# A hybrid decoder layer on one core: first loads and steps in another order, key tiles in turn with the gate logits, inverse roots spread without diagonal tiles

## The chip, the core and the metric

The kernel runs on one core of a Trainium2 chip. A core has a matrix engine (TensorE, PE in the profile, with its weight loads as PEld), a vector engine (VectorE, DVE), a scalar engine (ScalarE, ACT), GpSimd (POOL) and a queue for transfers (SyncE, SP). Each works through its own list of instructions in a fixed order and waits for the others by semaphores. The metric is the device time of one launch in microseconds (us), less is better.

## The reference

One decoder layer over 1024 prompt tokens and 8 x 8 sample tokens (1088 columns in the kernel), width 1024. Two branches work on the same normalized input and are merged by sigmoid gates; an MLP and a gated projection of per-layer inputs follow. All is float32.

```python
def trunk_layer(h, p_l, ...):
    proj = rmsnorm(h, norm_mix) @ w_in
    qkv, z, b_logit, a_logit, sq, sk, sv, gates = jnp.split(proj, cuts, axis=-1)
    o_a, conv_new, s_new = gdn_branch(qkv, z, b_logit, a_logit, ...)
    o_b, k_new, v_new = swa_branch(sq, sk, sv, ...)
    gates = jax.nn.sigmoid(gates)
    mix = gates[..., :D_MODEL] * o_a + gates[..., D_MODEL:] * o_b
    h = h + mix @ w_out
    hid = jax.nn.relu(rmsnorm(h, norm_ffn) @ w_up)
    h = h + (hid * hid) @ w_down
    h = h + jax.nn.sigmoid(rmsnorm(h, norm_ple) @ w_ple_gate) * (p_l @ w_ple_proj)
...
def gdn_branch(...):      # causal conv of width 4 with silu, then the gated delta rule in chunks of 64
    beta = jax.nn.sigmoid(b_logit)
    g = -jnp.exp(a_log) * jax.nn.softplus(a_logit + dt_bias)
...
def swa_branch(...):      # 16 heads of 64, 4 key heads, window of 128, sinks
```

## The kernel before, in words

Activations lie transposed: 128 channels on the partitions, tokens along the columns, in three column chunks (`CH`) of 384, 384 and 320. Each float32 product of a weight tile is made of three matmuls in a faster float type: high x high, high x low, low x high (`gemm_steps`, lines 165 to 167). So each weight tile `wr` that is loaded is split into `wh` (ScalarE, line 133) and `wl` (GpSimd, for the first two tiles VectorE, line 134). A list `order` holds the order of the weight tiles; `next_w` keeps the load three tiles and the split two tiles ahead. Activations are split in the same way (`xh` by ScalarE at line 316, `xl` by VectorE or GpSimd at line 317; `phi` and `plo` for the per-layer inputs, line 285).

Code is written in the order of the steps, and a scheduler with its own costs then fixes each engine's list. A generator given to `side` lets other work be set between the matmuls of a tile: after every third matmul (line 168) one entry of `side` is called.

The stages in the order of time: eight tiles of the per-layer projection, `ple(0)` to `ple(7)`, 18 matmuls each, whose results are copied to `ppo` (line 327) and stored; between them, `x_norm` for each of the three chunks of x, in three steps: squares (line 305) and folds (line 308) to one column sum per partition; `rsqrt_pe`; scaling (line 315) and splitting. Then 48 matmuls for the gate logits (line 385, weight `wba`), the gate arithmetic, the eight key tiles (`conv_steps`: 72 matmuls each, then a convolution with three VectorE steps at line 508 and the key at line 519, then `key_rows` and `key_products`), the tiles of the sliding-window branch, while VectorE solves the triangular systems (`substitute`, lines 657 and 658, tiles `fs` and `LT`). Then come eight gate tiles with the attention's steps between their matmuls: scores (lines 921 and 922, from `khi`, `klo` and `qst`), spreading (944), values (966); `qst` is made at line 892 and `klo` at line 879. The recurrent heads, the output projection, the MLP and the last gate follow.

`rsqrt_pe` turns column sums into inverse roots that lie on all partitions. One-column matmuls (line 246) bring the sums of up to 128 tokens into a column of `psn`; VectorE scales them (249), GpSimd takes the power (250); for each 128 tokens VectorE makes a diagonal tile `dg` (255, two buffers), and PE spreads it by a product with ones (256). It is called for the three chunks of x, and for the three chunks at the end of the output projection and of the MLP (`col_rsqrt_pe`, where PE's L246 waits for `acc`, line 1355).

Of the kernel before, what the change touches and what calls it, by code (L numbers as in the profile page):

```python
# [17 lines left out]
P = 128  # L18
# [20 lines left out]
def hybrid_layer(ctx: ExitStack, tc: tile.TileContext, d):  # L39
# [72 lines left out]
    wst = dict(raw=[], split=[], used=0)  # L112
# [8 lines left out]
    def w_split():  # L121
        i = len(wst["split"])
        if i < len(order):
            raw, n = wst["raw"][i]
            hi = wp.tile([P, 1024], F32R, name="wh", tag="wh")
            lo = wp.tile([P, 1024], F32R, name="wl", tag="wl")
            rv, hv, lv = raw[:, :n], hi[:, :n], lo[:, :n]
            if n == 128:

                rv = rv.rearrange("p (k m) -> p k m", m=16)  # L130
                both = hi[:, :256].rearrange("p (k m) -> p k m", m=32)
                hv, lv = both[:, :, 0:16], both[:, :, 16:32]
            act(hv, rv, AF.Copy)  # L133
            (nc.gpsimd if i > 1 else nc.vector).tensor_tensor(lv, rv, hv.bitcast(F32), ALU.subtract)  # L134
            wst["split"].append((hi, lo))

    def next_w():
        i = wst["used"]
        wst["used"] += 1
        while len(wst["raw"]) < min(i + 3, len(order)):  # L140
            w_load()
        while len(wst["split"]) < min(i + 2, len(order)):
# [94 lines left out]
    def rsqrt_pe(acc, c0, w, mul, add, rb, np_):  # L237
# [14 lines left out]
        for c in range(n):  # L252
            m = min(P, w - c * P)
            dg = np_.tile([P, P], F32, name="dg", tag="dg", bufs=2)
            ts(out=dg[:m, :m], in0=ident[:m, :m], scalar1=comp[:m, c : c + 1], scalar2=None, op0=ALU.mult)
            mm(ps[:, c * P : c * P + m], ones[:m], dg[:m, :m], start=True, stop=True)
# [4 lines left out]
    def col_rsqrt_pe(acc, mul, add, rb, np_):  # L261
        for c0, w in CH:
            rsqrt_pe(acc[:, c0 : c0 + w], c0, w, mul, add, rb, np_)
# [11 lines left out]
    with ExitStack() as st:  # L275
# [5 lines left out]
        for i, (c0, w) in enumerate(CH):  # L281
# [5 lines left out]
            if i == 0 or i == 1:  # L287
                w_load()
                w_split()
        for i, (c0, w) in enumerate(CH):  # L290
# [4 lines left out]
            if i == 1:  # L295
                load_constants()
        w_load()

        def x_norm(i):
# [6 lines left out]
            n = 4  # L306
# [4 lines left out]
            rs = rsqrt_pe(sq[:, 0], c0, w, 1.0 / 1024, EPS, None, pp)  # L311
# [23 lines left out]
        for step in (0, 1, 2, n0, n1, n0, n0, 3, n1, n2, n1, 4, 5, n2, n2, 6, 7):  # L335
# [11 lines left out]
    def evac_to(dst):  # L347
        def f(c0, w, ps):
            act(dst[:, c0 : c0 + w], ps[:, :w], AF.Copy)  # L349
        return f  # L350

# [28 lines left out]
    wb, _ = next_w()  # L380
    for c0, w in CH:
        ps = pg.tile([P, 512], F32, name="ps", tag="ps")
        for k in range(KT):
            for i in range(2):
                mm(ps[:32, :w], wb[:, k * 32 : k * 32 + 32], xs[k][i][:, c0 : c0 + w], start=(k + i == 0), stop=(k + i == KT))
        act(ba[:, c0 : c0 + w], ps[:32, :w], AF.Copy)
# [93 lines left out]
    def conv_tile(f, cvp, dst):  # L480
        st = conv_steps(f, cvp, dst)
        while True:
            try:
                next(st)
            except StopIteration as e:
                return e.value

    def conv_steps(f, cvp, dst):

        raw = cvp.tile([P, RAWW], F32, name="raw", tag="raw", bufs=2)  # L490
        rs = raw[:, 3 + NP :].rearrange("p (b t) -> p b t", t=11)
        nc.gpsimd.memset(raw[:, 0:3], 0.0)
        nc.gpsimd.tensor_copy(rs[:, :, 0:3], cache[:, f])

        def evac(c0, w, ps):
            n = min(w, NP - c0)
# [1037 lines left out]
```

## Time and profile before

| | us |
|---|---|
| runs: median of three | 2181.7 |
| runs: lowest, highest | 2180.86, 2184.86 |
| profiled execution: its own time | 2175.17 |
| profiled execution: span from the first to the last instruction | 2173.4 |
| PE busy in the span | 2111.1 |
| DVE, ACT, POOL busy | 1081.9, 796.6, 706.7 |

The mean granted clock of TensorE in the span is 0.986 of full speed. In the profile, L and a number is a line of the kernel; a tile's name stands with what it is made from (`wl<-wr,wh`). A row of the timeline gives the start, the length, the engine, the line and the operation, and in brackets the time that the engine stood idle ahead of it with what ended that. Rows of windows give the busy time of each engine in a stretch of time. A matmul's length holds its way through the array; two matmuls overlap, so their cost is read from their starts.

### The profile page before, as it was taken

The numbers are of one execution on the slowest core, as the hardware profiler recorded it, in microseconds if no ns is written. First come the engines' busy times: TensorE is split into PE (matmuls) and PEld (weight loads), VectorE is DVE, ScalarE is ACT, GpSimd is POOL, SyncE is SP. The second block draws the span as 40 slices with busy tenths as digits, with TensorE's granted clock in tenths as the row PEclk, the third lists the DMA queues.
The fourth block names the chain that finished last, engine by engine and source line by source line (L and its number), as shares of the span: only waits on it lengthen the run. The fifth ranks groups of instructions, "written<-read, shape, count | busy, mean of one in ns | idle before, by whom it ended". The sixth has DMA issues, their size and how long they took to land.

```text
span 2173.4 us, 33492 instructions
## 1 busy us (share of the span) xinstructions
PE 2111.1 (97%) x13485; PEld 2010.5 (93%) x13485; DVE 1081.9 (50%) x1724; ACT 796.6 (37%) x1951; POOL 706.7 (33%) x616
## 2 busy tenths in 40 slices
PE   7999998899999999999999999999999999999999
PEld 6899998777889999999998999999999999999999
DVE  6454599776644555455545543233332323333654
ACT  6576432576643443343335223122121212212321
POOL 4333355333234444544445321212121221212121
PEclk9999999999999999999999999999999999999999
DMA  6465343432143133222332221111111111111132
GB/s 245 140 202 186 106 154 104 128 118 91 64 139 101 64 98 121 94 73 86 111 112 78 88 89 40 39 49 42 46 49 39 49 39 49 47 42 49 39 125 80
DMA packets 89575, 196.62 MB, mean 90 GB/s; under 512 B 34124, under 2 KB 45260, under 8 KB 89292
## 3 DMA queue, kind: packets, MB, share of 16 engines
q1 hardware_dynamic: 89420, 194.48, 27.6%
q8 instruction: 106, 1.74, 0.3%
q14 instruction: 49, 0.40, 0.1%
HBM read 145.61 MB, written 50.78 MB: 90 GB/s over the span
## 4 chain that ended last, share of the span: by engine, by line
PE 80%; DVE 10%; ACT 4%; issue 3%; DMA 1%; POOL 1%; SPq 0%; DVEq 0%; ACTq 0%; POOLq 0%
PE ps L165 23%; PE ps L167 22%; PE ps L166 22%; DVE fs L657 3%; DVE LT L658 2%; PE psn L966 1%; PE pst L944 1%; PE psc L1252 1%; PE pst L1232 1%; PE psc L921 1%; ACT pst L568 1%; PE psc L1247 1%; PE psc L922 1%; PE pst L1126 1%; PE psn L1264 1%
## 5 line engine op out<-in xcount | busy, mean ns | idle before, releaser
L134 POOL TENSOR_TENSOR wl<-wr,wh 128x1024 fp32r<-128x1024 f32 x140 | 343.7, 2455 | 903.8 <-ACT wh L133 903.8
L165 PE MATMUL ps<-xh,wh 128*128 128x384 f32 (+1 forms) x1800 | 626.5, 348 | 3.0 <-ACT qf L349 1.6
L166 PE MATMUL ps<-xl,wh 128*128 128x384 f32 (+1 forms) x1800 | 597.6, 332 | 0.0
L167 PE MATMUL ps<-xh,wl 128*128 128x384 f32 (+1 forms) x1800 | 594.5, 330 | 0.0
L165 PEld LDWEIGHTS ps<-xh,wh 128*128 128x128 f32 x1800 | 341.2, 190 | 26.2 <-issue 21.0
L133 ACT ACTIVATE wh<-wr 128x1024 fp32r<-128x1024 f32 x143 | 150.8, 1054 | 526.1 <-PE ps L166 444.2
L166 PEld LDWEIGHTS ps<-xl,wh 128*128 128x128 f32 x1800 | 341.7, 190 | 1.6 <-issue 0.7
L167 PEld LDWEIGHTS ps<-xh,wl 128*128 128x128 f32 x1800 | 340.6, 189 | 1.9 <-issue 0.9
L165 PE MATMUL ps<-uh,wh 128*128 128x384 f32 (+1 forms) x768 | 250.7, 326 | 1.2 <-DVE h L1403 1.2
L167 PE MATMUL ps<-uh,wl 128*128 128x384 f32 (+1 forms) x768 | 250.9, 327 | 0.0
L166 PE MATMUL ps<-ul,wh 128*128 128x384 f32 (+1 forms) x768 | 250.6, 326 | 0.0
L1403 DVE TENSOR_TENSOR h<-h,ps 128x384 f32<-128x384 f32 (+1 forms) x192 | 100.6, 531 | 226.3 <-PE ps L167 226.3
L166 PE MATMUL ps<-pl,wh 128*128 128x384 f32 (+1 forms) x600 | 197.5, 329 | 0.0
L165 PE MATMUL ps<-ph,wh 128*128 128x384 f32 (+1 forms) x600 | 197.4, 329 | 0.0
L167 PE MATMUL ps<-ph,wl 128*128 128x384 f32 (+1 forms) x600 | 197.0, 329 | 0.0
L1389 DVE TENSOR_TENSOR ul<-us,uh 128x384 fp32r<-128x384 f32 (+1 forms) x96 | 98.0, 1022 | 115.3 <-ACT uh L1388 115.3
L165 PEld LDWEIGHTS ps<-uh,wh 128*128 128x128 f32 x768 | 144.1, 188 | 2.0 <-DVE h L1403 2.0
L167 PEld LDWEIGHTS ps<-uh,wl 128*128 128x128 f32 x768 | 144.1, 188 | 0.0
L166 PEld LDWEIGHTS ps<-ul,wh 128*128 128x128 f32 x768 | 144.1, 188 | 0.0
L508 DVE SCALAR_TENSOR_TENSOR cacc<-raw,cw,cacc 128x1112 f32<-128x1112 f32 x72 | 109.5, 1521 | 62.0 <-ACT cacc L506 56.7
L1387 ACT ACTIVATE us<-ut 128x384 f32<-128x384 f32 (+1 forms) x96 | 48.2, 502 | 197.6 <-DVE ut L1386 196.1
L1386 DVE SCALAR_TENSOR_TENSOR ut<-ps,rb 128x384 f32<-128x384 f32 (+1 forms) x96 | 51.3, 535 | 138.2 <-PE ps L167 138.2
(407 smaller groups left out, 3472.1 us busy)
## 6 DMA issues: line engine op xcount, KB each, us to landing
wr<-win SPq DMA_DIRECT2D x60, 512.0 KB
wr<-wup SPq DMA_DIRECT2D x32, 512.0 KB
wr<-wdn SPq DMA_DIRECT2D x32, 512.0 KB
ppd<-ppo SPq DMA_DIRECT2D x8, 544.0 KB
kTd<-kT SPq DMA_DIRECT2D x8, 544.0 KB
Ed<-E SPq DMA_DIRECT2D x8, 544.0 KB
rg<-Ed SPq DMA_DIRECT2D x8, 544.0 KB
gkT<-kTd SPq DMA_DIRECT2D x8, 544.0 KB
```

Source lines behind the costliest of these rows:

```text
L133: act(hv, rv, AF.Copy)
L134: (nc.gpsimd if i > 1 else nc.vector).tensor_tensor(lv, rv, hv.bitcast(F32), ALU.subtract)
L165: mm(ps[:M, :w], a, h[:, c0 : c0 + w], start=(k == 0), stop=False)
L166: mm(ps[:M, :w], a, l[:, c0 : c0 + w], start=False, stop=False)
L167: mm(ps[:M, :w], b, h[:, c0 : c0 + w], start=False, stop=(k == n - 1))
L508: stt(out=cc, in0=raw[:, j : j + CONVW], scalar=cw[:, f, j : j + 1], in1=cc, op0=ALU.mult, op1=ALU.add)
L657: tt(tmp, X[:, j : j + 1, j + 1 :].broadcast_to(sh), X[:, 0:j, j : j + 1].broadcast_to(sh), ALU.mult)
L658: tt(X[:, 0:j, j + 1 :], X[:, 0:j, j + 1 :], tmp, ALU.add)
L1386: stt(out=t, in0=ps[:, :w], scalar=0.0, in1=rb2[:, c0 : c0 + w], op0=ALU.max, op1=ALU.mult)
L1387: act(s, t, AF.Square)
L1389: tt(lo[:, c0 : c0 + w], s, hi[:, c0 : c0 + w].bitcast(F32), ALU.subtract)
L1403: tt(hc, hc, ps[:, :w], ALU.add)
```

## The change

1. First loads: the order was p0, wpp0, p1, wpp1, p2, x0, x1, constants, x2; now it is p0, wpp0, p1, p2, x0, constants, wpp1, x1, the first key weight, x2. `wba` moves behind the first two key weights in `order`, and its split goes to a tile of its own (`wn`).
2. In `x_norm`, the first fold (1536 columns) is done by GpSimd for the chunks 1 and 2. The steps come in the order 0, 1, 2, n0, 3, n0, n0, 4, n1, 5, n1, 6, n1, n2, 7, n2, n2.
3. `rsqrt_pe` has no diagonal tile: the column of inverse roots is broadcast along the free dimension as one operand, and the identity is the other.
4. The first two key tiles and the logits run chunk by chunk in turn: key 0, key 1, logits for the first two chunks, logits, key 0, key 1 for the third. The gate arithmetic comes behind them.
5. The attention's steps start at slot 20 of the gate tiles' slots instead of slot 6, with a second step in each tenth slot.

```diff
-    order = [(d["wpp"][u], 1024) for u in range(2)] + [(d["wba"], 128)]
+    order = [(d["wpp"][u], 1024) for u in range(2)]
     order += [(d["win"][f], 1024) for f in WIN_ORDER]
+    order.insert(4, (d["wba"], 128))
...
-            dg = np_.tile([P, P], F32, name="dg", tag="dg", bufs=2)
-            ts(out=dg[:m, :m], in0=ident[:m, :m], scalar1=comp[:m, c : c + 1], scalar2=None, op0=ALU.mult)
-            mm(ps[:, c * P : c * P + m], ones[:m], dg[:m, :m], start=True, stop=True)
+            mm(ps[:, c * P : c * P + m], comp[:m, c : c + 1].broadcast_to([m, P]), ident[:m, :m], start=True, stop=True)
...
+        p_chunk(0)
         w_load()
+        w_split()
+        p_chunk(1)
+        p_chunk(2)
+        x_chunk(0)
+        load_constants()
+        w_load()
+        w_split()
+        x_chunk(1)
+        w_load()
+        x_chunk(2)
...
-            n = 4
+            (tt if i == 0 else nc.gpsimd.tensor_tensor)(sq[:, 0:4], sq[:, 0:4], sq[:, 4:8], ALU.add)
+            n = 2
             while n:
                 tt(sq[:, 0:n], sq[:, 0:n], sq[:, n : 2 * n], ALU.add)
                 n //= 2
...
-        for step in (0, 1, 2, n0, n1, n0, n0, 3, n1, n2, n1, 4, 5, n2, n2, 6, 7):
+        for step in (0, 1, 2, n0, 3, n0, n0, 4, n1, 5, n1, 6, n1, n2, 7, n2, n2):
...
+    wst["narrow"] = lambda: kp.tile([P, 256], F32R, name="wn", tag="kb", bufs=1)
+
+    def logit_steps():
+        wb, _ = next_w(0)
+        for c0, w in CH:
+            ps = pg.tile([P, 512], F32, name="ps", tag="ps")
+            for k in range(KT):
+                for i in range(2):
+                    mm(ps[:32, :w], wb[:, k * 32 : k * 32 + 32], xs[k][i][:, c0 : c0 + w], start=(k + i == 0), stop=(k + i == KT))
+            act(ba[:, c0 : c0 + w], ps[:32, :w], AF.Copy)
+            yield
...
+    first = [conv_steps(8 + h, kp, key_tile) for h in range(2)]
+    logits = logit_steps()
+    for i, _ in enumerate(CH):
+        for st in (*first, logits) if i < 2 else (logits, *first):
+            next(st)
...
-                if n >= 6:
+                if n >= 20:
                     next(steps, None)
+                    if n % 10 == 9:
+                        next(steps, None)
```

Three places show what the scheduler makes of it. The first is GpSimd's list at the start; `rcomp` is the column of inverse roots, `xl` the low part of a normalized x tile (`xc_139` before and `xc_133` now are chunk 0, `xc_142` and `xc_152` chunk 1), `xsq` the squares. Before:

```order
L250 TENSOR_TENSOR rcomp<-rcomp,pwr 128x3 x2
L317 TENSOR_TENSOR xl<-xc_139,xh 128x384 x4
L134 TENSOR_TENSOR wh<-wr,wh 128x8x16
L317 TENSOR_TENSOR xl<-xc_139,xh 128x384 x2
L317 TENSOR_TENSOR xl<-xc_142,xh 128x384 x5
```

and now:

```order
L253 TENSOR_TENSOR rcomp<-rcomp,pwr 128x3
L318 TENSOR_TENSOR xsq<-xsq 128x1536
L330 TENSOR_TENSOR xl<-xc_133,xh 128x384 x2
L137 TENSOR_TENSOR wl<-wr,wh 128x1024
L330 TENSOR_TENSOR xl<-xc_133,xh 128x384 x4
L253 TENSOR_TENSOR rcomp<-rcomp,pwr 128x3
L318 TENSOR_TENSOR xsq<-xsq 128x4x320
L330 TENSOR_TENSOR xl<-xc_152,xh 128x384 x5
```

The power of chunk 1 stood right behind that of chunk 0; now the fold of chunk 1, six subtractions and a weight's split stand between them.

The second is VectorE's list around the first scores of the attention, within the triangular solution (`fs` and `LT`; the last number of an `LT` row counts down as it goes on). Before:

```order
L658 TENSOR_TENSOR LT<-LT,fs 128x49x14
L657 TENSOR_TENSOR fs<-LT 128x650
L892 TENSOR_TENSOR qst<-qraw,qst 64x1024
L658 TENSOR_TENSOR LT<-LT,fs 128x50x13
L879 TENSOR_TENSOR klo<-kraw,khi 128x1024
L657 TENSOR_TENSOR fs<-LT 128x612
```

and now:

```order
L687 TENSOR_TENSOR LT<-LT,fs 128x49x14
L686 TENSOR_TENSOR fs<-LT 128x650
L687 TENSOR_TENSOR LT<-LT,fs 128x50x13
L921 TENSOR_TENSOR qst<-qraw,qst 64x1024
L686 TENSOR_TENSOR fs<-LT 128x612
L908 TENSOR_TENSOR klo<-kraw,khi 128x1024
```

`qst` and `klo` each moved one operation of the solution back. On PE, 46 matmuls of the first gate tiles stand ahead of the first score, where 27 stood.

The third is PE's list at the end of the output projection, where the inverse roots are made; `psn` takes the column sums, `pst` the spread roots, and `ps` are plain matmuls. Before:

```order
L246 MATMUL psn<-cst,acc 128x1 x2
L246 MATMUL psn<-cst,acc 64x1
L165 MATMUL ps<-ph_12657,wh 128x384
L256 MATMUL pst<-dg,cst 128x128 x2
L166 MATMUL ps<-pl_12658,wh 128x384
L256 MATMUL pst<-dg,cst 128x128 x2
L167 MATMUL ps<-ph_12657,wl 128x384
L256 MATMUL pst<-dg,cst 128x128 x2
L165 MATMUL ps<-ph_12657,wh 128x384
L256 MATMUL pst<-dg,cst 128x64
```

and now:

```order
L257 MATMUL pst<-cst,rcomp 128x128 x6
L249 MATMUL psn<-cst,acc 128x1 x2
L249 MATMUL psn<-cst,acc 64x1
L169 MATMUL ps<-pl_12546,wh 128x320
L170 MATMUL ps<-ph_12545,wl 128x320
L168 MATMUL ps<-ph_12638,wh 128x384
L257 MATMUL pst<-cst,rcomp 128x128 x2
L257 MATMUL pst<-cst,rcomp 128x64
```

The spreading matmuls stood in twos between plain ones; now six come together ahead of the last column sums, and three behind three plain matmuls.

More of the change, by code (lines that the diff above doesn't have):

```diff
@@ L135, in w_split, with next_w @@
             wst["split"].append((hi, lo))
-    def next_w():
+    def next_w(ahead=1):
         i = wst["used"]
         wst["used"] += 1
-        while len(wst["raw"]) < min(i + 3, len(order)):
+        while len(wst["raw"]) < min(i + 2 + ahead, len(order)):
             w_load()
-        while len(wst["split"]) < min(i + 2, len(order)):
+        while len(wst["split"]) < min(i + 1 + ahead, len(order)):
             w_split()
```

134 lines of the change are left out of this document (65 added, 69 removed).

## The prediction

> **What bounds the kernel now.** I read the page first, for the engine that sets the time.
>
> ```profile
> PE 2111.1 (97%) x13485; PEld 2010.5 (93%) x13485; DVE 1081.9 (50%) x1724; ACT 796.6 (37%) x1951; POOL 706.7 (33%) x616
> ```
>
> TensorE (PE) is busy for 2111.1 of 2173.4 us, so no edit that leaves its matmuls alone can win more than the 62.3 us in which it stands, plus what it loses while it is busy at a lower clock. The second view is PE's waits (what it waited for, microseconds in all, times, longest).
>
> ```profile
> PE psc L921 <- DVE qst L892: 8.2, 1, 8.2
> PE ps L165 <- ACT wh L133: 6.7, 1, 6.7
> PE pst L256 <- DVE dg L255: 3.9, 2, 3.3
> PE ps L165 <- ACT ppo L327: 3.3, 1, 3.3
> PE psc L921 <- POOL qst L892: 2.3, 1, 2.3
> PE ps L165 <- ACT phi L285: 1.7, 1, 1.7
> PE pst L432 <- DVE lg L417: 1.7, 1, 1.7
> ```
>
> The 6.7 us are the first weight's load and split; the change keeps that load in place, so they stay. The other rows are what it can reach: 8.2 and 2.3 us in the attention, the rest at the start. The third view is the same places as windows (window, its length, busy time of PE, PEld, DVE, ACT and POOL with counts; then the granted PE clock, DMA share, GB/s).
>
> ```profile
> 28.00:36.00 8.00, 4.60 (x18) 4.04 (x17) 8.00 (x13) 5.69 (x14) 7.29 (x7) 0.69 0.33 111
> 36.00:46.00 10.00, 7.57 (x43) 7.22 (x41) 8.00 (x14) 5.90 (x15) 8.03 (x9) 0.91 0.62 218
> 46.00:52.00 6.00, 5.09 (x21) 4.38 (x22) 4.91 (x12) 2.22 (x6) 1.88 (x3) 0.72 0.00 1
> 60.00:88.70 28.70, 27.02 (x167) 25.69 (x167) 16.56 (x61) 12.62 (x38) 6.72 (x8) 1.00 0.25 80
> 367.00:376.00 9.00, 0.78 (x5) 0.49 (x4) 8.80 (x9) 0.69 (x1) 3.27 (x2) 0.79 0.00 0
> 420.00:440.00 20.00, 15.68 (x96) 12.68 (x96) 13.12 (x29) 10.23 (x29) 10.10 (x5) 0.74 0.42 120
> 1297.00:1311.00 14.00, 13.41 (x61) 12.12 (x60) 3.98 (x14) 1.42 (x3) 2.94 (x4) 0.63 0.09 34
> 2069.00:2081.00 12.00, 10.96 (x56) 9.90 (x55) 4.10 (x14) 1.42 (x3) 2.94 (x4) 0.72 0.35 134
> ```
>
> The window from 60 to 88.7 holds the gates' matmuls and the first two key tiles. Two things are lost in the others: idle time, and time at a clock of about a half. The two blocks of inverse roots (the last two rows) show almost no idle time: they lose by the clock, and by small matmuls that wait their turn. The fourth view is PE's own timeline at the start (start, length, what, and in brackets the wait ahead).
>
> ```profile
> 12.61 0.59 PE L165 MATMUL ps<-phi,wh 128*128 128x320 f32 x2 [1.69 <-ACT phi L285]
> 13.21 0.34 PE L167 MATMUL ps<-phi,wl 128*128 128x384 f32 x1
> 13.38 0.34 PE L165 MATMUL ps<-phi,wh 128*128 128x384 f32 x1
> ...
> 32.13 0.69 PE L165 MATMUL ps<-phi,wh 128*128 128x384 f32 x1 [3.35 <-ACT ppo L327]
> ...
> 34.54 0.52 PE L165 MATMUL ps<-phi,wh 128*128 128x384 f32 x1
> 34.86 0.52 PE L166 MATMUL ps<-plo,wh 128*128 128x384 f32 x1
> ...
> 46.90 0.68 PE L256 MATMUL pst<-dg,cst 128*128 128x128 f32 x4 [3.33 <-DVE dg L255]
> ```
>
> Starts of 384-column matmuls lie 0.17 us apart after the wait of 1.69 us, and 0.32 apart after the one of 3.35: the longer wait costs its own length and then some microseconds at half speed. In the Trainium skill, "TensorE: Matmul & The Clock Gate", Part 1, the clock halves after about one idle window of 3.4 us that runs freely; the 3.35 and 1.69 fit that, but the block at 1297 does not, since it shows a clock of 0.63 with 0.6 us idle. I therefore go by the granted clock of the rows.
>
> What the start loses now, by these rows: waits 1.7 + 3.35 + 3.33 + 1.7 = 10.1 us. The clock of 0.69 in 8 us and 0.91 in 10 us is (0.31 x 8 + 0.09 x 10) / 0.5 = 6.8 us at half clock, about 1.1 of them before the restart at 32.13, so some 5.7 us of work lost half its speed, 2.8 us; 0.72 in 6 us is 3.4 us, 1.7 lost. Together about 14.6 us.
>
> **The change part by part.**
>
> **First loads, POOL's fold, and the first steps.** These rows carry the costs (DVE's, then POOL's timeline).
>
> ```profile
> 20.58 1.75 DVE L308 TENSOR_TENSOR xsq<-xsq 128x1536 f32<-128x1536 f32 x1
> 26.58 1.66 DVE L315 SCALAR_TENSOR_TENSOR xc<-xc,par,pst 128x384 f32<-128x384 f32 x3
> 28.16 0.55 DVE L317 TENSOR_TENSOR xl<-xc,xh 128x384 fp32r<-128x384 f32 x1
> ```
>
> ```profile
> 20.75 2.31 POOL L250 TENSOR_TENSOR rcomp<-rcomp,pwr 128x3 f32<-128x3 f32 x1 [20.32 <-DVE rcomp L249]
> 25.49 0.85 POOL L250 TENSOR_TENSOR rcomp<-rcomp,pwr 128x3 f32<-128x3 f32 x1 [2.44 <-DVE rcomp L249]
> 39.32 5.22 POOL L317 TENSOR_TENSOR xl<-xc,xh 128x384 fp32r<-128x384 f32 x5 [1.97 <-ACT xh L316]
> 52.92 2.40 POOL L134 TENSOR_TENSOR wl<-wr,wh 128x1024 fp32r<-128x1024 f32 x1 [0.41 <-ACT wh L133]
> ```
>
> The third chunk of p now lands ahead of x0, and ScalarE copies it before x0's squares: the 1.69 us wait goes. The next thing late is x0. PE finishes tiles 0 to 3 at about 21 (72 matmuls of 0.16 from 6.65, with the first dozen at half speed), then has three column sums and stands for the power on POOL: 0.85 us if alone, 2.31 if it meets VectorE as at 20.75; I take 0.85.
>
> Tile 4 then runs to about 26.2, and after it PE's order has the column sums of x1, with its spreading matmuls right behind, ahead of tiles 5 to 7, which need neither. PE is in order, so 54 ready matmuls stand behind x1. Its first fold is now on POOL. No row shows that fold there: DVE takes 1.75 us for it, and POOL's 2.40 for 1024 columns makes 3.6 for 1536; I take 3.6, POOL's own rate. From about 23.4, where I lay the end of x1's squares (the constants are now loaded ahead of it), that ends at 27.0. The two remaining folds (each a part of 1.75: 0.9 and 0.5) are behind x0's eight scalings (8 x 0.55) and two subtractions (2 x 0.55) on DVE, 5.5 us from 23.9, so they end at about 30.8: PE waits some 4.5 us. Then the power of x1 has to wait on POOL behind six subtractions of x0 (5.22 / 5 = 1.04 each) and a weight's split (2.40), 8.7 us from 27.0, and ends about 36: PE stands another 4.3 us after its sums. x2's power costs a further 1.2 or so. Waits: 0.85 + 4.5 + 4.3 + 1.2 = 10.9 us, and about 2.3 us lost to half clock behind the middle two, as before behind one such wait. That is 13.2 against 12.9 before (14.6 without the gate chain's 1.7): the new order makes about as much standing time as it takes away. A second count, by stages, is kinder: laying tiles 5 to 7, then the 192 matmuls of two key tiles and the logits behind these waits, I reach about 82.6, to which the gates' matmuls, now behind, add about 4 with the 1.7 us wait; before, the same work was over at 88.7, where the last window of the start ends. That gives −2.
>
> **Gates behind the key tiles.** They run on DVE between the convolution's operations of the two key tiles, whose results PE wants next. The cover is the third key tile's matmuls. Bounds: the 1.7 us wait goes, or the chain comes 1.2 us late for the transposed keys and 2 us late for the cumulative sums. I take half of that, +1.6, against −1.7. Start in all: −2 by stages, 0.3 to the bad by waits: I take **−1 us**, from −8 (both waits on x1 gone: 8.8) to +4.
>
> **Attention later.** The rows around its first score (DVE, then POOL):
>
> ```profile
> 368.18 2.93 DVE L658 TENSOR_TENSOR LT<-LT,fs 128x720 f32<-128x720 f32 x1
> 374.37 1.22 DVE L892 TENSOR_TENSOR qst<-qraw,qst 64x1024 fp32r<-64x1024 f32 x1
> 375.62 0.84 DVE L658 TENSOR_TENSOR LT<-LT,fs 128x650 f32<-128x650 f32 x1
> ```
>
> ```profile
> 367.84 2.51 POOL L892 TENSOR_TENSOR qst<-qraw,qst 64x1024 fp32r<-64x1024 f32 x1
> ```
>
> The first score needs qst, which stands on DVE within the substitution. In the new order it comes behind one more of its steps, 0.84 us later; PE gets 46 gate matmuls ahead of the score where it had 27. The 19 more are 4 x 0.17 + 15 x 0.15 = 2.9 us. So the 8.22 us wait becomes 8.2 − 2.9 + 0.84 = 6.1: −2.1 us, still long enough for a half clock behind it. From 420 to 440 PE stands 20 − 15.68 = 4.3 us and the clock of 0.74 is 10.4 us at half, of which some 6 of work, 3 us lost: 7.3 us in all, from the end of the substitution through qst on POOL. One set of scores fewer lies on DVE ahead of that end, and in the other direction the steps are packed into fewer slots (189 calls against 186, with room for 198). Bounds −7 and +3; I take −1, near nothing, since the chain behind the substitution is untouched. Attention: **−3 us**, from −7 to +1.5.
>
> **Inverse roots without diagonal tiles.** PE's and POOL's rows in the block at 1297:
>
> ```profile
> 1300.51 1.05 PE L256 MATMUL pst<-dg,cst 128*128 128x128 f32 x4
> ```
>
> ```profile
> 1308.13 0.47 PE L165 MATMUL ps<-ph,wh 128*128 128x320 f32 x1
> ```
>
> ```profile
> 1302.84 1.21 POOL L250 TENSOR_TENSOR rcomp<-rcomp,pwr 128x2 f32<-128x2 f32 x2 [1.19 <-DVE rcomp L249]
> ```
>
> Between the first spreading matmul (1300.51) and the first plain matmul behind the block lie 7.6 us for some 4 us of work at full clock (my count, at 0.17 us for a plain matmul), in small portions: a diagonal tile can only be made when the last one but one has been read, so DVE and PE take turns. The nine new spreading matmuls have the shape of the old ones; what a broadcast stationary operand costs, no row shows. Bounds: nothing more, or twice the old ones (9 x about 0.3 us, 2.7 more). I take the old price, since operand and shape are alike. No turns are left: six run together after the power of two chunks, three after the last power, 1.21 us, with three plain matmuls ahead of them as cover. Laying this out ends the block about 2.7 us sooner at full clock; at the half clock that the row shows (0.63), where matmuls and not turns take the time, 1.5 to 2. I take 2, and twice that for two blocks: **−4 us**, from −1 to −10 (if the clock stays full as well, some 5 each: 0.63 in 14 us and 0.72 in 12 us lose 5.2 and 3.4 us by the clock alone).
>
> The moved `wba` split (a 128-column tile) goes off the load's path and costs nothing that PE sees: the logits now stand behind a key chunk each.
>
> **The sum.** −1 − 3 − 4 = −8 us. The profiled execution takes 2175.2 us (span 2173.4), 6.5 below the median of the runs shown, 2181.7, a gap of 0.3% that I leave as it is: 2167 profiled, and 2173.7 beside the median. About 0.2%, 4.4 us, is what a measurement of this kernel can tell from no change.
>
> **The rivals.**
>
> A, *the forecast*: the blocks get shorter by their turns, the attention's wait by 2 to 3 us, the start exchanges waits: 2173.7, from 2168 to 2179. Chance 0.46.
>
> B, *the clock stays full*: with fewer pieces between matmuls the granted clock in the two blocks stays near 1.00 (5 us each), and so in 420 to 440 (3 us); with attention's 2 and the start's 2 that is −17: 2165. For it: those windows lose by the clock with hardly any idle time. Against: the column sums that precede the spreading are still there, and the clock falls before the first of the old turns is over. Chance 0.22. By the skill's rule of idle windows (the page above) the blocks, with no wait near 3.4 us, should not have been slow at all; the rows show that they were, so it bears on this case little.
>
> C, *the waits only move*: the attention's PE wait comes back at its next set of scores, since the substitution on DVE ends when it ended, and the start gains nothing. Left are the blocks' 4: 2177.7. For it: all of DVE's 8.80 us of 9.00 in the window at 367 belongs to the substitution's stretch, which the change doesn't shorten. Chance 0.18.
>
> D, *x1 stands in POOL's queue* (slower): x1's fold on POOL meets VectorE's two-operand work. The row at 368.18 took 2.93 us where its like takes about 0.9, while POOL's qst ran from 367.84 to 370.35; the power at 20.75 took 2.31 for 0.85. If fold, six subtractions and split meet such company, the fold takes 3.2 us more and the power of x1 stands 3.5 us longer, PE waits some 15 us for x1 with a further 2 lost at half clock twice (4 us), and the gates come 3.2 us late: +14 on the start as laid out, less the 2 of stages: +12. With attention's −2 and the blocks' −4, +6: 2188. It decides when the power of x1 ends after about 42 us, against 36 in my layout. Against: most of x0's work on VectorE has one operand in PSUM, and the old order already kept POOL at these subtractions from 28 to 45 us. Chance 0.14. In the Trainium skill, "SBUF — State Buffer", "two separate sides", a VectorE instruction with two SBUF inputs and a GpSimd instruction lock each other out for a whole instruction. The row at 368.18 agrees: it ended 0.76 us after POOL's qst did. By that rule each of x0's two subtractions on DVE that meets the fold waits for it, or it for them, which is the mechanism of this rival.
>
> **How the numbers follow.** Faster by over 0.2% (under 2177.3): 0.9 of A, all of B, 0.4 of C: 0.41 + 0.22 + 0.07 = 0.70. Slower by over 0.2% (over 2186.1): 0.8 of D, 0.11. Between: 0.19. The range leaves out most of D and the far end of B: 2162 to 2185.
>
> **What would show it.** Right: no wait of 1.7 us at 12 us; two waits of PE of 3 to 6 us between 25 and 40 us, one for the fold's column sums and one for POOL's power; the wait for qst near 6 us; the blocks 1.5 to 3 us shorter, their clock still between 0.6 and 0.75. Wrong: x1's waits together over 12 us (D) or under 4 (the start gains far more); a clock near 1.00 in the blocks (B); a wait at the second set of scores as long as the 2 us that were saved (C). Broadcast spreading matmuls over twice 0.3 us would undo the third term.

## The result, and the profile after

The changed kernel takes 2188.17 us (median of 8 runs) beside 2179.03 us before (8 runs); the ratio is 1.0055, with a 95% interval of 1.0028 to 1.0081. It is slower by about half a per cent. The prediction was 2173.7, with a range of 2162 to 2185: the wrong side, and outside the range. It was laid beside a median of three runs, 2181.7; from the median of eight the same −8 us would give 2171. Its rival D had named 2188, but by a mechanism that did not make this loss, as will be seen. Two single runs further down took 7079.61 us (folds on VectorE, gates first) and 4063.72 us (the combined candidate); their ratios leave them out.

The profiled execution of the changed kernel has a span of 2193.7 us, 20.3 over the one of before. The medians differ by 9.1: the one profiled execution lies above its median, the other below; why single executions differ so much comes at the end of the experiments.

PE's waits after, those that bear on the change (what it waited for, microseconds in all, times, longest):

```profile
PE ps L168 <- ACT qf L362: 9.5, 1, 9.5
PE pst L973 <- ACT pr L960: 9.4, 14, 2.0
PE psn L249 <- DVE xsq L321: 8.6, 1, 8.6
PE ps L168 <- ACT wh L136: 6.8, 1, 6.8
PE psc L950 <- DVE qst L921: 6.2, 1, 6.2
PE psc L614 <- ACT kb L616: 4.9, 2, 3.0
PE pst L257 <- POOL rcomp L253: 3.0, 4, 1.2
PE ps L445 <- POOL wn L137: 2.7, 1, 2.7
```

and two of the kernel before:

```profile
PE psc L587 <- ACT kb L589: 2.1, 2, 1.2
PE ps L165 <- ACT qf L349: 1.6, 1, 1.6
```

The waits for `phi`, `ppo` and `dg` at the start are gone; one of 8.6 us for x1's column sums has come. The wait for `qst` is 6.2 us instead of 8.2. But the longest wait of all, 9.5 us, is for `qf` (query features that ScalarE copies out of PE's results), at the end of the key stage; it was 1.6 us before, and the prediction doesn't mention it. The wait for `kb` (the key products that ScalarE copies), within the key stage, has grown from 2.1 to 4.9 us. The waits for `pr` in the attention have grown too, from 3.9 to 9.4 us.

Where the time went is seen when the same stretches of both traces stand beside each other. Windows of the changed kernel (window, length, busy time of PE, PEld, DVE, ACT, POOL, then PE clock, DMA share, GB/s):

```profile
0.00:60.00 60.00, 41.95 (x226) 39.74 (x227) 34.55 (x50) 36.20 (x62) 30.95 (x28) 0.91 0.67 238
60.00:130.00 70.00, 64.57 (x410) 58.35 (x409) 30.94 (x75) 33.88 (x103) 19.96 (x30) 1.00 0.38 122
130.00:230.00 100.00, 94.34 (x592) 90.63 (x591) 47.00 (x47) 60.32 (x194) 30.73 (x31) 0.98 0.58 179
230.00:300.00 70.00, 57.87 (x355) 54.85 (x354) 43.86 (x88) 34.80 (x97) 30.57 (x21) 0.90 0.49 144
```

and of the kernel before:

```profile
0.00:60.00 60.00, 44.23 (x233) 38.56 (x234) 37.75 (x61) 35.86 (x67) 27.23 (x30) 0.91 0.68 238
60.00:130.00 70.00, 67.89 (x431) 65.02 (x431) 36.59 (x84) 42.82 (x141) 22.80 (x27) 1.00 0.47 156
130.00:230.00 100.00, 95.52 (x612) 91.86 (x610) 44.65 (x55) 61.77 (x197) 29.25 (x31) 1.00 0.60 189
230.00:300.00 70.00, 68.45 (x422) 66.81 (x423) 52.88 (x83) 28.86 (x69) 35.91 (x24) 0.98 0.49 147
```

From 60 to 300 us PE's busy time is 3.3 + 1.2 + 10.6 = 15.1 us less than before, so it stands that much longer, and it loses by the clock besides (0.90 for 0.98 in the last 70 us, and 0.98 for 1.00 in the hundred before). The first matmul of the third key tile, by which time the projection, the logits and two key tiles are done in both kernels, starts at 87.36 us after and 89.48 before: up to there the change is 2.1 us ahead. But the kernel before has also done 16 matmuls of the gate arithmetic and 8 transposes of the first key by then, which take it 4 to 5 us with the 1.7 us wait among them, and the changed kernel has them still to come: in this pair of profiles the start itself has won nothing. The first matmul of the norms that follow the key stage starts at 249.42 and 230.38: 19.0 us behind. The first score comes at 394.68 instead of 375.73 (19.0 behind), the first column sum of the first block of inverse roots at 1319.04 instead of 1298.14 (20.9), the end 20.3. So the loss arises between 87 and 250 us, in the key stage, and in this pair of profiles everything later hardly changes it. From the first matmul of the third key tile to the norms the stage takes 162.1 us, beside 140.9 before.

What is late there? Four rows of VectorE in the changed kernel: a step of the first key's convolution, ahead of which VectorE stood idle for 25.89 us; the first row of the gate arithmetic; its end (`g`); and the first decay tile `E`, which is made from `g` by way of a store and a load.

```profile
85.94 1.94 DVE L394 SCALAR_TENSOR_TENSOR cacc<-raw,cw,cacc 128x1112 f32<-128x1112 f32 x1 [25.89 <-ACT cacc L392]
87.80 0.28 DVE L468 COPY lg<-pst 128x64 f32<-128x64 f32 x2
103.35 0.21 DVE L489 SCALAR_TENSOR_TENSOR g<-lg,ea 128x64 f32<-128x64 f32 x1
117.55 1.23 DVE L582 TENSOR_TENSOR E<-E,cst 128x1024 f32<-128x1024 f32 x1 [1.35 <-DMA E<-gcd]
```

The last three in the kernel before:

```profile
61.05 0.29 DVE L398 COPY lg<-pst 128x64 f32<-128x64 f32 x2 [5.37 <-PE pst L427]
68.12 0.22 DVE L419 SCALAR_TENSOR_TENSOR g<-lg,ea 128x64 f32<-128x64 f32 x1
82.92 1.22 DVE L555 TENSOR_TENSOR E<-E,cst 128x1024 f32<-128x1024 f32 x1
```

The gate arithmetic begins 26.8 us later, because PE transposes the logits only at 86.71 us, behind the two key tiles; and it takes 15.6 us to `g` instead of 7.1, because steps of two convolutions stand between its rows. So `g` is 35 us later, and so is the first of eight decay tiles. One `E` is needed for each head's products `kk` and `kb`, and a chain runs through the heads, of ScalarE's and VectorE's work and two transfers. From the first `E` to the eighth it takes 136.8 us before (to 219.68) and 125.3 after (to 242.81): the chain catches up by 11.5 of its 35 us. That fits VectorE's waits for the start of a convolution, which hangs on PE's matmuls: between 82 and 245 us they are 33.6 us before and 49.7 − 25.9 = 23.8 after. The eighth `E` is left 23.1 us late. In the kernel before, ScalarE was done with the last `kb` at 224.52, stood 3.04 us for PE behind it and took `qf` at 228.63: the chain had a lead of 4.1 us.

```profile
223.64 0.88 ACT L589 ACTIVATE kb<-psc 64x256 f32<-64x256 f32 x2
228.63 0.49 ACT L349 ACTIVATE qf<-ps 128x384 f32<-128x384 f32 x1
```

With that lead used up, 23.1 − 4.1 = 19.0 us are left, and by these the norms are late. The end of the chain in the changed kernel (GpSimd, VectorE, ScalarE and PE in the order of time):

```profile
237.15 2.35 POOL L137 TENSOR_TENSOR wl<-wr,wh 128x1024 fp32r<-128x1024 f32 x1 [9.94 <-ACT wh L136]
```

```profile
242.81 1.23 DVE L582 TENSOR_TENSOR E<-E,cst 128x1024 f32<-128x1024 f32 x1
```

```profile
244.07 2.44 ACT L587 ACTIVATE E<-E,ngc 128x128 f32<-128x128 f32 x8 [6.08 <-DMA kksd<-kd]
246.42 0.33 ACT L588 ACTIVATE E<-E,ngcs 64x64 f32<-64x64 f32 x1
246.77 0.87 ACT L616 ACTIVATE kb<-psc 64x256 f32<-64x256 f32 x2
247.67 0.49 ACT L362 ACTIVATE qf<-ps 128x384 f32<-128x384 f32 x1
```

```profile
248.21 0.69 PE L168 MATMUL ps<-xh,wh 128*128 128x384 f32 x1 [9.46 <-ACT qf L362]
```

ScalarE empties PE's buffers in its own fixed order, and there the eighth head's exponentials and `kb` stand ahead of `qf`. It stands idle for 6.08 us, until `E` is there (the row names a transfer, but VectorE ends `E` at 244.04, and ScalarE starts at 244.07); PE, which waits for a buffer, stands behind it. `E` itself stands on VectorE behind small steps that wait for a power of GpSimd's (over at 241.56), and that stands behind the weight's split, the first row above.

### The profile page after: what moved, and what is told of

It is laid out like the page before. It is cut to its first block, busy times and chain, and to the rows that moved or that the text cites. A ratio compares the mean times of both kernels' runs of the same rounds, so it can differ in the third digit from the quotient of the medians.

```text
span 2193.7 us, 33440 instructions
## 1 busy us (share of the span) xinstructions
PE 2110.4 (96%) x13485; PEld 2008.9 (92%) x13485; DVE 1081.8 (49%) x1695; ACT 798.4 (36%) x1951; POOL 713.5 (33%) x618
## 4 chain that ended last, share of the span: by engine, by line
PE 75%; DVE 9%; issue 2%; ACT 2%; POOL 1%; DMA 0%; DVEq 0%; ACTq 0%; POOLq 0%
PE ps L168 21%; PE ps L170 21%; PE ps L169 21%; DVE LT L687 3%; DVE fs L686 3%; PE psn L995 1%; PE pst L973 1%; PE psc L1283 1%; PE pst L1263 1%; PE pst L1157 1%; PE psc L1278 1%; PE psc L950 1%; PE psc L951 1%; PE psn L1295 1%; PE psc L1288 1%
## 5 line engine op out<-in xcount | busy, mean ns | idle before, releaser
L168 PE MATMUL ps<-xh,wh 128*128 128x384 f32 (+1 forms) x1800 | 627.4, 349 | 10.9 <-ACT qf L362 9.5
L394 DVE SCALAR_TENSOR_TENSOR cacc<-raw,cw,cacc 128x1112 f32<-128x1112 f32 x72 | 115.0, 1598 | 74.9 <-ACT cacc L392 73.1
```

The source lines that it names most:

```text
L168: mm(ps[:M, :w], a, h[:, c0 : c0 + w], start=(k == 0), stop=False)
L394: stt(out=cc, in0=raw[:, j : j + CONVW], scalar=cw[:, f, j : j + 1], in1=cc, op0=ALU.mult, op1=ALU.add)
```

## The experiments

The theories. **G**: the gate arithmetic behind two key tiles makes `E` late, and the key stage's chain ends late. **S**: not the gates but the tiles' turns do it, since two convolutions meet on VectorE. **A**: the later attention does it. All ratios below are to the kernel before, on the same chip.

### The changed kernel with logits and gates first again

```diff
-    first = [conv_steps(8 + h, kp, key_tile) for h in range(2)]
-    logits = logit_steps()
...
+    wb, _ = next_w()
+    for c0, w in CH:
+        ps = pg.tile([P, 512], F32, name="ps", tag="ps")
...
```

> The changed kernel with the logits and the gate arithmetic back ahead of the key tiles (part 4 undone), all else as changed. Theory G (the gate arithmetic behind the two key tiles makes the first decay tile E late: read at 113 us instead of 75.5, and the products of the key stage end some 18 us later): the loss between 120 and 250 us is gone, PE's wait for qf near 250 us is under 3 us instead of 9.5, time 2174 to 2181 beside 2179 before. Rival A (the later attention costs the time): still 2185 to 2190.

Measured: 2176.13 us, ratio 0.9994 (0.9977 to 1.0011). `g` is ready at 69.63 us, the norms' first matmul is at 234.79, and the wait for `qf` is 1.6 us, as before the change. A falls: the later attention is still in this kernel. All of the loss that can be measured lies in part 4, with the move of the logit weight that belongs to it.

### The changed kernel with the gates ahead of the third chunk of the key tiles

```diff
-        for st in (*first, logits) if i < 2 else (logits, *first):
+        for st in (*first, logits) if i < 2 else (logits,):
             next(st)
...
         if h < 2:
             st = first[h]
+            next(st)
```

> The changed kernel with the two key tiles and the logits still in turn, but the third chunk of the logits and the gate arithmetic ahead of the third chunk of the two key tiles. Theory G: the first E is read near 80 us again, and the time comes to 2172 to 2180, below the changed kernel by 8 to 16. Rival S (not the gates: two convolutions at once on VectorE make the keys of head 0 late, 96 us instead of 87): E early, but PE still waits for kb and qf, 2184 to 2190.

Measured: 2180.63 us, ratio 1.0012 (0.9994 to 1.0030). `g` comes at 88.24, not as early as I had expected, and the first `E` is used at 104.06 instead of near 80; the norms' first matmul is at 238.61, the wait for `qf` is 1.6 us. With the turns kept, and only the gates moved, the time falls by 7.5 us, a little less than the expected 8. The first key is as late here as in the changed kernel (99.9 us beside 96.2, and 86.8 before), and yet the key stage takes 145.2 us, beside 140.9 in the kernel ahead. G explains most of the loss, S at most these 4.3 us, of which late gates are again a part.

### The kernel before with key tiles and logits in turn alone

```diff
+    for i, _ in enumerate(CH):
+        for st in (*first, logits) if i < 2 else (logits, *first):
+            next(st)
```

> The kernel before with part 4 alone (key tiles and logits in turn, gates behind, the logit weight behind two key weights). Theory G and rival S alike: 12 to 20 us slower than before, 2191 to 2199, with the wait for qf over 7 us. Rival A: no difference to before, within 3 us of 2179.

Measured: 2190.5 us, ratio 1.0067 (1.0043 to 1.0090): 11.6 us slower, just under the 12 to 20 that were expected. Its own waits show the same picture:

```profile
PE psc L941 <- DVE qst L912: 9.1, 1, 9.1
PE ps L168 <- ACT qf L353: 8.0, 1, 8.0
PE psc L605 <- ACT kb L607: 7.5, 4, 4.0
```

Part 4 alone is as slow as the whole change (the intervals overlap); the other parts together make no difference that can be measured (0.9994 in the first experiment).

### The kernel before with the gates late, and no turns

```diff
-    for i, _ in enumerate(CH):
-        for st in (*first, logits) if i < 2 else (logits, *first):
+    for st in (logits, *first):
+        for _ in CH:
             next(st)
```

The lines in which it differs are shown against the kernel of the experiment ahead; the logit weight has its old place.

> The kernel before with one thing changed: logits, then the first two key tiles one after the other as before, and only then the gate arithmetic. Theory G: the first E is read 25 to 40 us later than before (75.5), and the time is 6 to 12 us over that of before: 2185 to 2191. Rival S (the tiles' turns, not the gates): within 3 us of before.

Measured: 2189.19 us, ratio 1.0045 (1.0026 to 1.0064): 10.3 us slower, with the tiles one after the other as before. `g` comes at 97.61, the first `E` at 111.42, PE waits 5.0 us for `qf`. This is the experiment that tells G from S: the turns are not needed for the loss, late gates alone make it. The first key is not late here (81.4 us), the first `E` is. What no run takes apart is the lateness of `E` and the place that the gate arithmetic takes in VectorE's list among the convolutions; that `E` is what counts is read from the rows above, where ScalarE waits for it.

Put side by side, the profiles of these kernels show how much the stage could take up (us in each profile; three profiles of the kernel before and of the changed one, from the last experiment below). The second column says how long after the start of the third key tile the first `E` is made, the third how long the key stage takes, from there to the norms' first matmul; the last is the median of the runs.

| kernel | first `E` | key stage | time |
|---|---|---|---|
| before | −6.6, −6.6, −6.6 | 140.9, 140.9, 140.9 | 2179.0 |
| logits and gates first | −5.2 | 140.9 | 2176.1 |
| gates ahead of the third chunk | 10.6 | 145.2 | 2180.6 |
| before, gates late, no turns | 26.2 | 154.6 | 2189.2 |
| before, in turn | 29.6 | 165.9 | 2190.5 |
| changed | 30.2, 31.1, 29.9 | 162.1, 163.0, 162.5 | 2188.2 |

An `E` that comes 17 us later against PE's work costs the stage 4 us, one that comes 33 us later 14, and one 36 to 37 us later 21 to 25 (in the last three kernels the gates' matmuls and the first key's transposes, some 3 us, lie in the stage too). Both columns come back in every profile of a program to about 1 us. Times since the launch do not: the norms' first matmul is at 230.4, 230.0 and 237.3 us in the three profiles of the kernel before. The stage is 21 to 22 us longer in the changed kernel, and the medians are only 9.1 apart, with an interval of 6 to 18 us; the three profiled executions are 16 apart on average. Some 3 us of the difference are the matmuls that moved into the stage; whether anything takes more back is not shown.

### The later attention alone

```diff
-                if n >= 6:
+                if n >= 20:
                     next(steps, None)
+                    if n % 10 == 9:
+                        next(steps, None)
```

> The kernel before with part 5 alone (attention's steps from slot 20, a second one in each tenth slot). The prediction's term was 3 us faster. Theory G, from the shift between the two traces over the gate tiles: the wait for qst falls by 2 us and later waits grow by as much or more, 0 to 4 us slower, 2179 to 2183. Rival A: 8 to 10 us slower, 2187 to 2189.

Measured: 2174.51 us, ratio 0.9986 (0.9970 to 1.0001). My theory had 0 to 4 us slower, which was wrong; the prediction's term of 3 us faster is the middle of the interval (0.14%), which just reaches no change. The wait for `qst` fell to 5.4 us.

```profile
PE pst L944 <- ACT pr L931: 6.8, 12, 2.0
PE psc L921 <- DVE qst L892: 5.4, 1, 5.4
PE psc L921 <- DVE pr L925: 4.0, 3, 2.4
```

The waits of the steps that follow have grown (for `pr`, from 3.9 and 2.1 to 6.8 and 4.0 us) by more than the one wait fell: this is the mechanism of rival C, and PE's waits do not show where a gain would come from.

### The changed kernel without the later attention

```diff
-                if n >= 20:
+                if n >= 6:
                     next(steps, None)
-                    if n % 10 == 9:
-                        next(steps, None)
```

> The changed kernel with part 5 undone. The prediction had part 5 at 3 us faster, the run of part 5 alone gave 4 faster: then this is 3 to 5 us slower than the changed kernel (2188), 2191 to 2193. If the late triangular solution of the changed kernel takes the gain back, it is the same as the changed kernel, within 2 us.

Measured: 2186.46 us, ratio 1.0030 (1.0011 to 1.0049). It is not slower than the changed kernel (1.0028 to 1.0081): in the changed kernel part 5 gains nothing that can be measured. There the triangular solution ends at 417.7 us instead of 400.7, so the late key stage reaches on to it. That this takes a gain back is an inference from the two ends; the intervals overlap.

### The start alone

The diff of parts 1 and 2 as shown, without the logit weight's move.

> The kernel before with parts 1 and 2 alone (first loads without the logit weight's move, steps, folds of chunks 1 and 2 on GpSimd). The prediction's stage count: 1 to 2 us faster. Rival P (x1 stands in GpSimd's queue): 3 us slower or more, with PE's wait for x1's column sums over 8 us.

Measured: 2184.86 us, ratio 1.0028 (1.0010 to 1.0045). Slower, against the prediction's −1 us. The diagonal tiles are still there: with the new steps PE waits 9.1 us for them, and 5.1 for `ppo`. One diagonal tile, 0.29 us alone, took 3.04 us (26.28 to 29.32) beside GpSimd's fold (25.82 to 29.24). Rival P's sign, a wait of over 8 us for x1's column sums, did not come: all waits for column sums of x are 0.7 us here.

```profile
PE pst L256 <- DVE dg L255: 9.1, 4, 4.7
PE psc L932 <- DVE qst L903: 8.3, 1, 8.3
PE ps L165 <- ACT wh L133: 6.4, 1, 6.4
PE ps L165 <- ACT ppo L338: 5.1, 1, 5.1
```

### The spreading without diagonal tiles alone

```diff
-            dg = np_.tile([P, P], F32, name="dg", tag="dg", bufs=2)
-            ts(out=dg[:m, :m], in0=ident[:m, :m], scalar1=comp[:m, c : c + 1], scalar2=None, op0=ALU.mult)
-            mm(ps[:, c * P : c * P + m], ones[:m], dg[:m, :m], start=True, stop=True)
+            mm(ps[:, c * P : c * P + m], comp[:m, c : c + 1].broadcast_to([m, P]), ident[:m, :m], start=True, stop=True)
```

> The kernel before with part 3 alone (no diagonal tiles). The prediction's term: 4 us faster in the two blocks, plus the 3.3 us wait at 47 us that goes. Theory from the two traces (in the blocks PE is busy with its own matmuls at about half clock, and the turns with VectorE lay beside other matmuls): the blocks within 1 us each of before, and at most the start's wait to win: 0 to 4 us faster, 2175 to 2179.

Measured: 2181.74 us, ratio 1.0008 (0.9992 to 1.0024): no gain, where the prediction had 4 us in the blocks alone, and my own expectation 0 to 4. At the start the waits for `dg` (3.9 us) are replaced by waits for the power on GpSimd:

```profile
PE pst L254 <- POOL rcomp L250: 9.5, 3, 5.9
```

So parts 1 and 2 lose by themselves, and part 3 gains nothing, by the same place: with the steps of before, the spreading now waits for a power that stands late; with the new steps the diagonal tiles are late. Together (the first experiment, with part 5) they cost nothing that can be measured.

### Folds on VectorE, gates first

```diff
-            (tt if i == 0 else nc.gpsimd.tensor_tensor)(sq[:, 0:4], sq[:, 0:4], sq[:, 4:8], ALU.add)
+            tt(sq[:, 0:4], sq[:, 0:4], sq[:, 4:8], ALU.add)
```

> Gates first, first loads and steps as changed, attention and spreading as changed, but all folds on VectorE again. In PE's list two more tiles of the projection now stand ahead of x1's column sums. If the wait of 7.7 to 8.6 us for those sums is the start's cost, it falls under 4 us and the time is 3 to 7 us under the run with gates first (2176), 2169 to 2173. If the wait only moves to the chain behind it, within 2 us of 2176.

Measured: 2175.65 us, ratio 0.9982 (0.9962 to 1.0003), the same as with the folds on GpSimd (2176.13). The wait for the column sums is gone, but a wait of 4.8 us for `ppo` stands in its place, and waits for the power of 3.1 us: it only moved.

### The changed kernel with folds on VectorE

The same edit in the changed kernel.

> The changed kernel with the folds of chunks 1 and 2 on VectorE again. If the gates' lateness is the bound of the whole stage behind, what the start wins is won in full or is lost in the key stage's waits: 0 to 5 us under the changed kernel, 2183 to 2188; theory G says that the wait for qf stays over 6 us.

Measured: 2184.56 us, ratio 1.0029 (1.0010 to 1.0048). The wait for `qf` is 6.1 us. The fold's engine is worth a few microseconds at most; its interval and that of the changed kernel overlap.

### The combined candidate

First loads, steps and later attention as changed, folds on VectorE, diagonal tiles kept, logits and gates first.

> A candidate: first loads, steps and the later attention as changed, folds on VectorE, diagonal tiles kept, logits and gates first. If what each part does alone adds up (attention 4 us faster, fold on VectorE about 1 faster), 2171 to 2175 beside 2179 before; if the diagonal tiles' wait at the start comes back, 2176 to 2180.

Measured: 2176.3 us, ratio 0.9980 (0.9961 to 0.9999). It beats before by about 0.2%, just clear of no change, and no more than the later attention alone does. The parts don't add up: PE waits 5.8 us for the diagonal tiles and 5.1 for `ppo` at the start.

### The spreading matmuls twice

```diff
-            mm(ps[:, c * P : c * P + m], comp[:m, c : c + 1].broadcast_to([m, P]), ident[:m, :m], start=True, stop=True)
+            for _ in range(1 if rb is None else 2):
+                mm(ps[:, c * P : c * P + m], comp[:m, c : c + 1].broadcast_to([m, P]), ident[:m, :m], start=True, stop=True)
```

> The kernel before with part 3, and every spreading matmul of the two blocks made twice (18 instead of 9 in each; those at the start once). If PE's own work at half clock bounds the blocks (the theory after the two traces), the 9 more cost 0.4 us each: 3.5 us per block, the first block's first column sum to the end 3 to 4 us longer, the time 5 to 8 us over part 3 alone (2181.7). If turns and waits bounded them (the prediction's step), the extra matmuls lie in gaps: under 2 us in all.

Measured: 2179.55 us, ratio 0.9997 (0.9979 to 1.0014). My expectation of 5 to 8 us more failed: no difference that the runs show. In the trace the nine extra matmuls lengthen the second block from 8.8 us (the changed kernel's, with the same 3.4 us at half clock) to 10.9, 0.23 us each, half of what I had put. That is 4 us for both blocks, which the two intervals, each about 7 us wide, can hide. The blocks did turn out to differ by the clock much more than by their work, which led to the next runs.

### The same two programs, profiled again

No edit: the changed kernel and the one before, two more executions each.

> The changed kernel again, for another profile. If the clock belongs to the program: 0.63 in the first block and 0.86 in the second once more, 10.4 and 8.8 us to the twelfth plain matmul. If it belongs to the execution: another pair, such as 1.00 and 7.7. The wait for qf (9.5 us) and the first E (117.5 us) stay within 0.3 us either way.

> The changed kernel a third time. By the execution theory, a third value of the clock in the blocks for the same program; by the other, 0.63 and 0.86 again.

> The kernel before again. Program: 0.63 and 0.72, 10.0 and 9.6 us. Execution: another pair. At a clock of 1.00 the diagonal tiles take 7.3 us in a block, as in the combined candidate, against 7.7 without them.

> The kernel before a third time. By the execution theory, another value of the clock in the blocks for the same program; by the other, 0.63 and 0.72 again.

Measured, from the first column sum of a block to its twelfth plain matmul (first and second block): changed 10.3 and 8.8 us in the first profile, 10.3 and 8.8 in the second, 8.8 and 7.7 in the third. Before: 10.0 and 9.6, then 9.8 and 8.3, then 7.3 and 7.3. The last one's windows over the two blocks:

```profile
1310.00:1324.00 14.00, 13.28 (x85) 11.82 (x84) 5.05 (x17) 2.30 (x5) 2.95 (x4) 1.00 0.08 32
2078.00:2090.00 12.00, 10.80 (x71) 9.64 (x71) 3.70 (x14) 1.42 (x3) 2.92 (x4) 1.00 0.34 130
```

Beside them the same windows of the changed kernel's first profile:

```profile
1318.00:1332.00 14.00, 13.43 (x60) 11.98 (x59) 1.52 (x5) 1.42 (x3) 2.95 (x4) 0.63 0.08 32
2090.20:2102.20 12.00, 10.43 (x60) 9.71 (x60) 1.62 (x5) 1.42 (x3) 2.91 (x4) 0.86 0.34 133
```

The program alone does not settle the clock in a block: the second profile of the changed kernel repeats the first, but the third does not, and the kernel before, with its diagonal tiles, runs both blocks at a clock of 1.00 in one execution and at 0.63 and 0.72 in another. And where the clocks are equal, the new spreading is not faster: 7.3 us with diagonal tiles against 7.7 without at a clock of 1.00 (the changed kernel's third profile, and its variants without the later attention and with folds on VectorE, 7.66 to 7.74), 8.3 against 8.8 with 3.4 us at half clock, 10.0 against 10.3 at 0.63. The waits, in contrast, came back: the changed kernel waits 9.4 and 9.5 us for `qf` in the two further profiles. The first `E` did not stay within 0.3 us of 117.5: it came at 121.08 in the second profile and at 117.80 in the third, since the start before it took longer in the second; against the third key tile it stayed within 0.9 us.

## Why the prediction was wrong, by its own steps

**Gates behind the key tiles.** This is the step that failed. The prediction priced it by the local waits (the gate chain 1.2 us late for the transposed keys, 2 us late for the cumulative sums) and took +1.6, with "the third key tile's matmuls" as cover. Locally that was about right: PE waits 1.53 us for `kT` and 0.97 for `emid`, and the third key tile's matmuls cover the rest. What was missed is who else waits for the gates: the decay tiles, the head of a chain of eight links. Of the 35 us by which this head came late, the chain caught up 11.5, its lead over PE took 4.1, and for the other 19 PE was late; the bill came 130 us later, at a place of which the prediction quoted no row, as `qf` and `kb`. In time the price is about 10 us (1.0045 for the lateness alone, 1.0067 with the turns). The rest of the miss is in the terms below: with logits and gates first, where only part 4 is undone, the time is 0.9994 of before, and not the some 8 us less that the other terms were to bring.

**The first loads and steps.** The mechanism was right, and mostly the sizes. The wait for `phi` went (one of 1.4 us stands in the changed kernel's second profile). By stages the layout had the two key tiles and the logits over at 82.6 us; they are over at 86.7. PE's waits for x came to 0.55 + 8.56 + 1.20 + 0.84 = 11.2 us, where the layout had 10.9, though otherwise shared: the sums waited 8.6 us, not 4.5, and the power 1.2, not 4.3. The fold on GpSimd took what the prediction had put (3.6):

```profile
23.70 3.49 POOL L318 TENSOR_TENSOR xsq<-xsq 128x1536 f32<-128x1536 f32 x1 [0.45 <-ACT xsq L317]
36.92 0.87 POOL L253 TENSOR_TENSOR rcomp<-rcomp,pwr 128x3 f32<-128x3 f32 x1
```

But rival D's mechanism did work on VectorE:

```profile
25.85 1.75 DVE L330 TENSOR_TENSOR xl<-xc,xh 128x384 fp32r<-128x384 f32 x1
27.53 2.18 DVE L328 SCALAR_TENSOR_TENSOR xc<-xc,par,pst 128x384 f32<-128x384 f32 x4
29.63 2.52 DVE L330 TENSOR_TENSOR xl<-xc,xh 128x384 fp32r<-128x384 f32 x1
```

The two subtractions, 0.55 us alone, took 1.75 and 2.52: the first was over 0.4 us after GpSimd's fold, the second 0.4 after its weight split (29.38 to 31.73). These 3.2 us are most of the 4 that the sums are later than laid out; the two folds behind them took 2.49 us, where the layout had 1.4, beside GpSimd's next subtractions. "SBUF — State Buffer" of the Trainium skill, "two separate sides", says that a VectorE instruction with two SBUF inputs and a GpSimd instruction that reads SBUF exclude each other for a whole instruction. These rows agree. Rival D's point of decision, the power of x1 over after 42 us, wasn't reached: it ended at 37.8. D was right on the time by accident.

**No wait was foreseen for `wn`.** The prediction said that the moved logit weight's split costs nothing that PE sees. PE waited 2.7 us for it at 63.27. The split came with the logits, and nothing covers it there.

**The attention.** Its term fits what this part gives alone (−3 us forecast, −0.14% measured, no change just within the interval), but no gain of it is measurable in the changed kernel. The wait for `qst` came out as forecast (6.2 us, 6.1 forecast); what followed moved as rival C had it.

**The inverse roots.** The step "no turns are left" failed: the turns with VectorE lay beside plain matmuls and cost nothing. At equal clocks the blocks are 0.3 to 0.5 us longer without diagonal tiles, where 4 us less for both were forecast. The 4 us forecast came from comparing a block at half clock with an ideal, and the clock is not the change's to give; rival B rested on the same error. In the Trainium skill, "TensorE: Matmul & The Clock Gate", Part 1, the window that sets the clock runs freely; that fits one program that finds different clocks. The recorded idle time does not tell these executions apart: PE's waits for `acc` at the two blocks are 1.6 to 1.7 us in all in every one of the six profiles, at clocks from 0.63 to 1.00.

## What to carry to other kernels

When a chain is moved back, look for its last consumer and not for its next one: list who reads its results, and how much later each of them may come, over the whole stage. A chain that shows no wait in the profile is hidden by slack, and slack has an amount: here a delay of 17 us cost the stage 4 us, and one of 37 us cost it 21 us, and the kernel about 10. And before a stretch is priced by a clock below 1.00, ask for a second execution of the same program.

## What was not expected of the hardware

The granted clock of the same instructions differs between executions of one program: 0.63 or 1.00 in blocks of column sums and spreading matmuls with nearly no idle time, worth 2.7 us in the first block of the kernel before. The cause of the drop in a block without idle time stays open: none of the runs changes the column sums.
